# Moving the cache_win row copies from the FFN to the projections, and re-ordering the start of a trunk layer

## The chip, the cores and the metric

The kernel runs on one core of a Trainium2 chip. The core has five engines that work side by side: TensorE (PE, matmuls), VectorE (DVE), ScalarE (ACT), GpSimd (POOL) and SyncE (SP, which here issues most DMAs). Each engine takes its instructions in order; engines wait for each other by semaphores. The metric is the device time of one execution in microseconds (us), the median over runs.

## The reference

One inference step of one trunk layer, for a prompt of 512 tokens and 8 samples of 4 tokens each, 544 tokens in all, width 1024, in float32:

```
adaLN modulation from silu(c) @ w_ada                     # per sequence
h = modulate(rmsnorm(x))
p = h @ w_in       # conv B, C, x_in | q | 3 kinds of k,v | gate | merge
y_a = B * conv3(C * x_in)
y_b = compressed + selected + sliding-window attention, gated per head
x = x + g1 * (merge(y_a, y_b) @ w_out)
x = x + g2 * swiglu(modulate(rmsnorm(x)))                 # 2816 wide
y = rmsnorm(x)
```

The samples read paged caches of 1024 past rows. The compressed branch passes blocks of 32 cached rows through a small MLP called phi. Outputs are y, the new cache rows, and for each sample the window cache `new_win_sample`: the old 512 rows of `cache_win` moved up by four, with four new rows at the end.

## The kernel before, in words

**Precision and linears.** A float32 matrix is used as a pair of float32r matrices, high and low part. A linear is three matmuls per 128 rows of k (`mm3`, L180 to L183): wh with x_hi, wh with x_lo, wl with x_hi. Tokens go in two halves of 288 and 256 columns. Weights arrive as 1 MB slabs of 256 output columns (`slab`, tile `raw`, three buffers); each half of a slab is split by `split`: ACT writes wh (L176), DVE then writes wl (L177). wh and wl have two buffers each, so a split can run while the linear before uses the other buffer, and must wait until the linear two before has ended.

**Order.** The order of instructions on each engine is set by a list scheduler, which models durations and DMAs and picks by time and priority; `tc.issue_after(x)` tells it to place what follows behind x. On the chip the order is then fixed. SP's queue is in order too: a DMA that waits for data holds up every DMA behind it, and each waits for the completion of the one eight before it.

**Stages.** (1) `wake`: transposes of the identity on PE while the first data arrive. (2) A loop of 16 steps n: `cmp_gather` reads 1 MB of cache_cmp pages by an indirect DMA on POOL's queue, two steps ahead; `cmp_copy` re-orders it on DVE (two copies to `gt2`); `cmp_T` transposes it on PE and splits it into xh (ACT) and xl (DVE); `cmp_M` multiplies by the phi weights. Those weights (`rphi`) are split in quarters by `phi_split` into wph (ACT) and wpl (DVE). Between the steps stand the adaLN slabs (`mod_slab`), the token rows (`x_rows`), the norm and `modulate`. (3) `kv_type` 0, 1, 2: six slabs of k and v projections. Of each half, ACT copies the result to `kvT`; `kv_post`, which follows one half later, transposes it on PE (`kvt`, `sps`), copies it to `stage` and `rows`, splits k into kh and kl and stores all these; at the end of types 1 and 2 ACT spreads the v rows into `vext`. `cmp_prompt` stands between types 1 and 2 (results `pps`, then `ph1` on ACT). (4) One gate slab (`gT`) and the q projections (tiles `rq`, results qh and ql, stored to `q_dr`). (5) The convolution and the samples' attention, whose selected rows are gathered from cache_sel in 2 MB pieces (`sraw`); (6) merges and prompt attention; (7) the output projection; (8) the FFN: a loop over c2 in which each pass takes a w_gate slab and a w_up slab, and leaves silu(gate) * up in `ffg`, split by ACT and DVE into f_hi and f_lo; (9) the down projection and the final norm.

**The cache rows.** `win_shift(b)` copies 508 rows of one sample from cache_win to new_win_sample, a DMA of 1 MB from DRAM to DRAM on SP's queue that touches no engine. The eight of them stand in the FFN loop, one behind the slabs of each pass c2 = 1 to 8 (L1338, called at L1348).

Of the kernel before, what the change touches and what calls it, by code (L numbers as in the profile page):

```python
# [9 lines left out]
F32 = mybir.dt.float32  # L10
# [9 lines left out]
KC = 8  # L20
TP = 512
# [4 lines left out]
DEC_B = 8  # L26
# [73 lines left out]
def build(tc, a, o):  # L100
    nc = tc.nc
    sync, act, dve, pool, pe = nc.sync, nc.scalar, nc.vector, nc.gpsimd, nc.tensor
# [28 lines left out]
    def nm(s):  # L131
        uid[0] += 1
        return f"{s}_{uid[0]}"
# [28 lines left out]
    last_slab = [None]  # L162
# [223 lines left out]
    perow = wphip.tile([32, 128], F32, name="perow")  # L386
    rws = []
# [26 lines left out]
    def wake():  # L414

        p = tp_ps("wake")
        for n in range(44):
            pe.transpose(p[:, (n % 4) * 128:(n % 4) * 128 + 128], ident, ident)
# [71 lines left out]
    gts.append(cmp_gather(0, 1))  # L490
# [6 lines left out]
    for j in range(4):  # L497
        sync.dma_start(xr[j], a["x_prompt"][j * 128:(j + 1) * 128, :])
# [34 lines left out]
    for n in range(16):  # L533
# [9 lines left out]
        if n == 0:  # L543
            phi_split(1, 0)
        if n < 3:
            for v in range(2):
                phi_split(v, n + 1)
        with tc.issue_after(last_x[0].ins), tc.issue_after(last_x[1].ins):
            if n == 0:
                pp = tp_ps("pep")  # L550
                pe.transpose(pp[:, 0:32], perow, ident[0:32, 0:32])
                dve.tensor_copy(peT[:, 0:32], pp[:, 0:32])
                vp = tp_ps("vp")
                pe.transpose(vp[:, 0:104], vrow, ident[0:104, 0:104])
                dve.tensor_copy(vec, vp[:, 0:104])
# [14 lines left out]
            if 1 <= n < 9:  # L570
                mod_slab(n - 1)
            if 3 <= n < 7:
                x_rows(n - 3)
            if n == 7:
                iv = inv_from_sums(ss1, xp)
                iv2 = xp.tile([128, 3], F32, name="iv2")
                dve.tensor_copy(iv2[:, 0:2], iv[:, 0:2])
                dve.tensor_copy(iv2[:, 2:3], iv[:, 4:5])
                invs = (inv_bcast(iv2, 0, xp), inv_bcast(iv[:, 2:4], 1, xp))
            if n == 9:  # L580
                modp.pop()()
                make_A(n1T, sc1, A1)
                mods = [modulate(xT, invs[hf], A1, sh1, hh_, hl_, hf, xp) for hf in range(2)]
            if 9 <= n < 13:
                for g_ in mods:
                    for _ in range(2):
                        next(g_)
        if n == 13:
            with tc.issue_after(last_slab[0].ins):
                sync.dma_start(x_dr, xT.rearrange("p k n -> p (k n)"))  # L590
            xst.close()
# [6 lines left out]

    def kv_type(ty, rp, x32=None):
        sps = acc_ps(nm("sps"))  # L600
        for v in range(2):
            sl = slab(a["w_in"], C_KV + ty * 512 + v * 256)
            stage = rp.tile([128, 4, 256], F32, tag="stage", bufs=2, name=nm("stage"))
# [97 lines left out]
    pool.memset(qbd, 0.0)  # L701
    for gp in range(2):
        for rp_ in range(2):
# [5 lines left out]
            for r2 in range(2):  # L709
# [3 lines left out]
                hl = [rp.tile([128, TP], F32R, tag=f"q{n}", bufs=2, name=nm("q" + n)) for n in "hl"]  # L713

# [10 lines left out]
                for n in range(2):  # L725
                    sync.dma_start(q_dr[gp][n][:, r * TP:(r + 1) * TP], hl[n].bitcast(F32))
# [609 lines left out]
    def win_shift(b):  # L1336
        flat = lambda z: z.rearrange("t w -> (t w)").rearrange("(p f) -> p f", p=128)
        sync.dma_start(flat(o["new_win_sample"][b, 0:508, :]), flat(a["cache_win"][b, 4:512, :]))  # L1338

# [5 lines left out]
    for c2 in range(1, FC // 2):  # L1345
        sg, su = slab(a["w_gate"], c2 * 256), slab(a["w_up"], c2 * 256)
        if c2 <= DEC_B:
            with tc.issue_after(last_slab[0].ins):  # L1348
                win_shift(c2 - 1)
# [110 lines left out]
```

## Time and profile before

| | |
|---|---|
| median of 3 runs | 1359.87 us (1359.06 to 1360.66) |
| profiled execution | 1358.56 us |
| its span | 1356.7 us |
| PE busy | 1315.6 us (97%) |
| DVE, ACT, POOL busy | 653.4, 538.8, 69.5 us |
| mean granted clock of PE | 0.991 |
| DMA traffic | 193.56 MB, 143 GB/s on average |

The span runs from the first to the last instruction that the profiler recorded; the time has 1.9 us around it. Busy times are of one engine each and overlap. In rows of the timeline the columns are the start, the duration, engine, line, operation, output and inputs, and in brackets the idle time of that engine just before and what ended it. In rows of windows they are start and end, length, busy time (and count) of PE, its weight loads, DVE, ACT and POOL, then the granted clock, the mean busy share of the DMA engines and GB/s.

### The profile page before, as it was taken

How to read it: one execution, taken by the hardware profiler on the slowest of the kernel's cores; microseconds unless marked ns; L12 is line 12 of the kernel's file. 1: busy time of each engine (PE TensorE's matmuls, PEld its weight loads, DVE VectorE, ACT ScalarE, POOL GpSimd, SP SyncE). 2: the span in 40 equal slices, each digit the busy share in tenths (PEclk: the TensorE clock that was granted, in tenths of full speed). 3: DMA queues.
4: the chain of work that ended last, by engine and by line, in shares of the span. 5: the costliest groups of instructions: out<-in, count | busy, mean ns of one | idle time of the engine just before them, and what ended most of it. 6: DMA issues, size and time to landing. Idle time of an engine off the chain costs nothing.

```text
span 1356.7 us, 25742 instructions
## 1 busy us (share of the span) xinstructions
PE 1315.6 (97%) x10884; PEld 1213.6 (89%) x10884; DVE 653.4 (48%) x1570; ACT 538.8 (40%) x1066; POOL 69.5 (5%) x123
## 2 busy tenths in 40 slices
PE   6999999999999999999999999999998999999997
PEld 5787799999999998998777778999998999999997
DVE  4457522244455454327667666657333232323335
ACT  3445333433333335226677666425222222222223
POOL 2001040000111010001000000000000000000000
PEclk7999999999999999999999999999999999999998
DMA  8785123953555443843637337422352243133321
GB/s 265 276 292 178 63 79 112 321 161 127 187 179 223 158 156 126 205 124 127 170 109 192 109 100 205 137 75 94 106 174 93 93 155 94 56 86 86 86 63 66
DMA packets 138024, 193.56 MB, mean 143 GB/s; under 512 B 4817, under 2 KB 124761, under 8 KB 132918
## 3 DMA queue, kind: packets, MB, share of 16 engines
q1 hardware_dynamic: 133302, 149.98, 35.8%
q0 software_dynamic: 4608, 41.95, 8.4%
q8 instruction: 85, 1.39, 0.4%
q14 instruction: 29, 0.24, 0.1%
HBM read 174.47 MB, written 25.76 MB: 148 GB/s over the span
## 4 chain that ended last, share of the span: by engine, by line
PE 94%; DVE 2%; ACT 1%; DMA 1%; issue 1%; SPq 0%; POOL 0%; ACTq 0%; POOLq 0%; DVEq 0%
PE lin L181 19%; PE lin L183 19%; PE lin L182 19%; PE dn L181 3%; PE dn L182 3%; PE dn L183 3%; PE acc L1145 3%; PE ptp L1151 3%; PE phi L458 2%; PE phi L460 2%; PE phi L459 2%; PE xt L444 2%; PE modp L229 2%; PE kt L862 2%; PE sp L1120 1%; PE sp L1121 1%
## 5 line engine op out<-in xcount | busy, mean ns | idle before, releaser
L181 PE MATMUL lin<-h_hi,wh 128*128 128x288 f32 (+1 forms) x1648 | 479.6, 291 | 11.5 <-ACT wh L176 11.5
L183 PE MATMUL lin<-h_hi,wl 128*128 128x288 f32 (+1 forms) x1648 | 473.3, 288 | 2.4 <-DVE wl L177 2.4
L182 PE MATMUL lin<-h_lo,wh 128*128 128x288 f32 (+1 forms) x1648 | 474.8, 289 | 0.0
L181 PEld LDWEIGHTS lin<-h_hi,wh 128*128 128x128 f32 x1648 | 311.1, 189 | 22.0 <-ACT wh L176 12.7
L183 PEld LDWEIGHTS lin<-h_hi,wl 128*128 128x128 f32 x1648 | 309.5, 188 | 4.1 <-DVE wl L177 3.8
L182 PEld LDWEIGHTS lin<-h_lo,wh 128*128 128x128 f32 x1648 | 310.7, 189 | 0.5
L177 DVE TENSOR_TENSOR wl<-raw,wh 128x1024 fp32r<-128x1024 f32 x132 | 158.5, 1205 | 217.6 <-ACT wh L176 217.3
L176 ACT ACTIVATE wh<-raw 128x1024 fp32r<-128x1024 f32 x132 | 137.1, 1043 | 276.3 <-PE lin L182 186.0
L181 PE MATMUL dn<-f_hi,wh 128*128 128x256 f32 (+1 forms) x352 | 101.9, 290 | 0.0
L182 PE MATMUL dn<-f_lo,wh 128*128 128x256 f32 (+1 forms) x352 | 101.3, 288 | 0.0
L183 PE MATMUL dn<-f_hi,wl 128*128 128x256 f32 (+1 forms) x352 | 101.0, 287 | 0.0
L1127 ACT ACTIVATE P<-P,nms 128x512 f32<-128x512 f32 (+3 forms) x128 | 70.6, 555 | 18.8 <-DVE nms L1126 18.1
L1126 DVE CUSTOM_DVE_ANT_0 P<-sp,ta 128x512 f32<-128x512 f32 (+3 forms) x128 | 57.6, 482 | 31.1 <-PE sp L1114 23.5
L183 PEld LDWEIGHTS dn<-f_hi,wl 128*128 128x128 f32 x352 | 66.3, 188 | 0.0
L181 PEld LDWEIGHTS dn<-f_hi,wh 128*128 128x128 f32 x352 | 66.2, 188 | 0.0
L182 PEld LDWEIGHTS dn<-f_lo,wh 128*128 128x128 f32 x352 | 66.2, 188 | 0.0
L1302 DVE TENSOR_TENSOR ffg<-lin,ffg 128x288 f32<-128x288 f32 (+1 forms) x44 | 19.4, 441 | 84.0 <-PE lin L183 84.0
L458 PE MATMUL phi<-xh,wph 128*128 128x512 f32 x128 | 54.1, 423 | 4.3 <-ACT xh L446 4.3
L459 PE MATMUL phi<-xh,wpl 128*128 128x512 f32 x128 | 51.9, 406 | 0.0
L460 PE MATMUL phi<-xl,wph 128*128 128x512 f32 x128 | 51.4, 403 | 0.0
L447 DVE TENSOR_TENSOR xl<-xt,xh 128x512 fp32r<-128x512 f32 x64 | 41.2, 684 | 17.1 <-ACT xh L446 16.9
L446 ACT ACTIVATE xh<-xt 128x512 fp32r<-128x512 f32 x64 | 34.8, 595 | 36.5 <-PE xt L444 35.6
(372 smaller groups left out, 2133.5 us busy)
## 6 DMA issues: line engine op xcount, KB each, us to landing
raw<-in_w_in SPq DMA_DIRECT2D x26, 1024.0 KB, 6.3
raw<-in_w_ada SPq DMA_DIRECT2D x24, 1024.0 KB, 6.0
raw<-in_w_gate SPq DMA_DIRECT2D x11, 1024.0 KB, 5.5
raw<-in_w_up SPq DMA_DIRECT2D x11, 1024.0 KB, 5.3
wraw<-in_cache_win POOLq DMA_DIRECT2D x8, 1024.0 KB, 6.9
raw<-in_w_down SPq DMA_DIRECT2D x8, 1024.0 KB, 5.6
out_new_win_sample<-in_cache_win SPq DMA_DIRECT2D x8, 1016.0 KB, 7.5
rq<-in_w_in SPq DMA_DIRECT2D x8, 512.0 KB, 6.8
```

Source lines behind the costliest of these rows:

```text
L176: act.activation(oh, view, AF.Copy)
L177: dve.tensor_sub(ol, view, oh.bitcast(F32))
L181: pe.matmul(p, lhsT=wh[:, k, :], rhs=xh, start=start, stop=False)
L182: pe.matmul(p, lhsT=wh[:, k, :], rhs=xl, start=False, stop=False)
L183: pe.matmul(p, lhsT=wl[:, k, :], rhs=xh, start=False, stop=stop)
L447: last_x[1] = dve.tensor_sub(xlb[v][:, lp * 512:lp * 512 + 512], p, xo.bitcast(F32))
L458: pe.matmul(po, lhsT=w_h, rhs=mh, start=first, stop=False)
L459: pe.matmul(po, lhsT=w_l, rhs=mh, start=False, stop=False)
L460: pe.matmul(po, lhsT=w_h, rhs=ml, start=False, stop=last)
L1126: dve.tensor_tensor_reduce(out=t[:, 0:n], in0=sps[br], in1=t_dist[:, 512 - n:512], scale=-hs, scalar=3e38, op0=ALU.add, op1=ALU.min, accum ...
L1127: act.activation(t[:, 0:n], t[:, 0:n], AF.Exp, scale=-1.0, bias=nms[:, c:c + 1], accum_out=sums[:, c:c + 1])
L1145: pe.matmul(acc[br * 64:br * 64 + 64, :], lhsT=vtok[br][:, j, g * 64:(g + 1) * 64], rhs=pts_[br], start=(j == 0), stop=False)
```

## The change

At the start: forty more identity transposes in `wake`; the second gather of cache_cmp is issued behind a small POOL copy that waits for the first one's data; the phi splits of a step are tied behind the splits of the gathered rows of that step; the x_prompt rows are loaded in steps 3 to 6 instead of at the start; the adaLN slabs, the token rows, the norm and modulate move two to four steps later. Further on: the copies win_shift(0) to (5) are issued behind the six k and v slabs, (6) and (7) behind stores of the q projections, and none in the FFN.

```diff
@@ -384,6 +384,7 @@
     sel = wphip.tile([128, 1], F32, name="sel")
     pbias = wphip.tile([128, 2], F32, name="pbias")
     perow = wphip.tile([32, 128], F32, name="perow")
+    gate = wphip.tile([128, 1], F32, name="gate")
     rws = []
 
     def phi_load(v):
@@ -414,7 +415,7 @@
     def wake():
 
         p = tp_ps("wake")
-        for n in range(44):
+        for n in range(84):
             pe.transpose(p[:, (n % 4) * 128:(n % 4) * 128 + 128], ident, ident)
 
     xhb = [gat.tile([128, 1026], F32R, name=f"xh{j}") for j in range(2)]
@@ -487,15 +488,14 @@
     sync.dma_start(perow, a["pe_cmp"].rearrange("v l d -> (v l d)").rearrange("(k p) -> k p", p=128))
     sync.dma_start(w2, a["w_phi2"].rearrange("v p d -> p v d"))
     phi_load(1)
-    gts.append(cmp_gather(0, 1))
+    with tc.issue_after(pool.tensor_copy(gate, gts[0][:, 0:1]).ins):
+        gts.append(cmp_gather(0, 1))
     for r0, nme, n in ((24, "b_ada", 48), (0, "norm1", 8), (8, "norm2", 8), (16, "norm_f", 8), (72, "b_conv", 8), (80, "w_conv", 24)):
         s = a[nme]
         s = s.rearrange("a b -> (a b)") if len(s.shape) == 2 else s
         sync.dma_start(vrow[r0:r0 + n, :], s.rearrange("(k p) -> k p", p=128))
     sync.dma_start(xs, a["x_sample"])
     sync.dma_start(strow, a["state_conv"])
-    for j in range(4):
-        sync.dma_start(xr[j], a["x_prompt"][j * 128:(j + 1) * 128, :])
 
     dve.tensor_reduce(sel, ident.rearrange("p (a b) -> p b a", b=32)[:, 0, :], axis=AX.X, op=ALU.add)
     dve.memset(peT[:, 32:64], 0.0)
@@ -540,12 +540,12 @@
             if pend is not None:
                 cmp_step(*pend)
             pend = (bp, qt, v)
-        if n == 0:
-            phi_split(1, 0)
-        if n < 3:
-            for v in range(2):
-                phi_split(v, n + 1)
         with tc.issue_after(last_x[0].ins), tc.issue_after(last_x[1].ins):
+            if n == 0:
+                phi_split(1, 0)
+            if n < 3:
+                for v in range(2):
+                    phi_split(v, n + 1)
             if n == 0:
                 pp = tp_ps("pep")
                 pe.transpose(pp[:, 0:32], perow, ident[0:32, 0:32])
@@ -567,25 +567,28 @@
                     phi_bias(v)
             if n == 2:
                 x_rows(4)
-            if 1 <= n < 9:
-                mod_slab(n - 1)
-            if 3 <= n < 7:
-                x_rows(n - 3)
-            if n == 7:
+            if 3 <= n < 11:
+                mod_slab(n - 3)
+            if 6 <= n < 10:
+                x_rows(n - 6)
+            if n == 10:
                 iv = inv_from_sums(ss1, xp)
                 iv2 = xp.tile([128, 3], F32, name="iv2")
                 dve.tensor_copy(iv2[:, 0:2], iv[:, 0:2])
                 dve.tensor_copy(iv2[:, 2:3], iv[:, 4:5])
                 invs = (inv_bcast(iv2, 0, xp), inv_bcast(iv[:, 2:4], 1, xp))
-            if n == 9:
+            if n == 11:
                 modp.pop()()
                 make_A(n1T, sc1, A1)
                 mods = [modulate(xT, invs[hf], A1, sh1, hh_, hl_, hf, xp) for hf in range(2)]
-            if 9 <= n < 13:
-                for g_ in mods:
-                    for _ in range(2):
-                        next(g_)
-        if n == 13:
+                steps = [g_ for _ in range(KC) for g_ in mods]
+            if n >= 11:
+                for _ in range(4 if n == 11 else 3):
+                    next(steps.pop(0))
+        if 3 <= n < 7:
+            with tc.issue_after(last_slab[0].ins):
+                sync.dma_start(xr[n - 3], a["x_prompt"][(n - 3) * 128:(n - 2) * 128, :])
+        if n == 15:
             with tc.issue_after(last_slab[0].ins):
                 sync.dma_start(x_dr, xT.rearrange("p k n -> p (k n)"))
             xst.close()
@@ -596,10 +599,16 @@
     outs_p = (o["new_cmp_prompt"], o["new_sel_prompt"], o["new_win_prompt"])
     outs_s = (o["new_cmp_sample"], o["new_sel_sample"])
 
+    def win_shift(b):
+        flat = lambda z: z.rearrange("t w -> (t w)").rearrange("(p f) -> p f", p=128)
+        sync.dma_start(flat(o["new_win_sample"][b, 0:508, :]), flat(a["cache_win"][b, 4:512, :]))
+
     def kv_type(ty, rp, x32=None):
         sps = acc_ps(nm("sps"))
         for v in range(2):
             sl = slab(a["w_in"], C_KV + ty * 512 + v * 256)
+            with tc.issue_after(last_slab[0].ins):
+                win_shift(ty * 2 + v)
             stage = rp.tile([128, 4, 256], F32, tag="stage", bufs=2, name=nm("stage"))
             for gp in range(2):
                 dst = rp.tile([128, NT], F32, tag="kvT", bufs=2, name=nm("kvT"))
@@ -699,6 +708,7 @@
     dve.tensor_copy(gtok, p[:, 0:192].rearrange("p (i f) -> p i f", i=4))
 
     pool.memset(qbd, 0.0)
+    last_q = [None]
     for gp in range(2):
         for rp_ in range(2):
             t = raw_tile("rq")
@@ -711,6 +721,9 @@
                 ch = gp * 4 + r
                 w = split(tv[:, :, :, r2 * 64:(r2 + 1) * 64], perm=lambda z: z.rearrange("p k (g f) -> p k g f", g=2))
                 hl = [rp.tile([128, TP], F32R, tag=f"q{n}", bufs=2, name=nm("q" + n)) for n in "hl"]
+                if ch in (1, 3):
+                    with tc.issue_after(last_q[0].ins):
+                        win_shift(6 + ch // 2)
 
                 def ev(hf, p):
                     src = p[:, TS:288] if hf == 0 else p
@@ -723,7 +736,7 @@
                             dve.tensor_scalar_mul(qbd[pr, :, gp, gg * 16 + r * 4:gg * 16 + r * 4 + 4], p[pr, 0:TS].rearrange("p (b t) -> p b t", t=4), 0.125)
                 linear(w, h, ev)
                 for n in range(2):
-                    sync.dma_start(q_dr[gp][n][:, r * TP:(r + 1) * TP], hl[n].bitcast(F32))
+                    last_q[0] = sync.dma_start(q_dr[gp][n][:, r * TP:(r + 1) * TP], hl[n].bitcast(F32))
     rst.close()
     p0.close()
 
@@ -1333,10 +1346,6 @@
             if hf == 0:
                 next(nh)
             ffn_up(c, g_, w[1], hf)
-    def win_shift(b):
-        flat = lambda z: z.rearrange("t w -> (t w)").rearrange("(p f) -> p f", p=128)
-        sync.dma_start(flat(o["new_win_sample"][b, 0:508, :]), flat(a["cache_win"][b, 4:512, :]))
-
     wxst.close()
     n2st.close()
     f6b = mkpool(f6st, "f6b", side="right")
@@ -1344,9 +1353,6 @@
         ffn_tiles(f6b, c)
     for c2 in range(1, FC // 2):
         sg, su = slab(a["w_gate"], c2 * 256), slab(a["w_up"], c2 * 256)
-        if c2 <= DEC_B:
-            with tc.issue_after(last_slab[0].ins):
-                win_shift(c2 - 1)
         for cc in range(2):
             c, g_ = c2 * 2 + cc, ffg()
             for v, fn in ((sg, lambda w, hf: ffn_gate(g_, w, hf)), (su, lambda w, hf: ffn_up(c, g_, w, hf))):
```

What the scheduler makes of it shows in the order of rows on each engine. First ACT at the end of the k and v projections of type 1, from the last evacuations of that type to the first slab of type 2 (wh_287 and wh_296 are its two halves). Before:

```order
L606 ACTIVATE kvT_261_2136<-lin_264_2141 128x288
L176 ACTIVATE wh_287_2363<-raw_284_2359 128x1024
L606 ACTIVATE kvT_261_2136<-lin_265_2167 128x256
L606 ACTIVATE kvT_269_2208<-lin_272_2213 128x288
L176 ACTIVATE wh_296_2458<-raw_284_2359 128x1024
L606 ACTIVATE kvT_269_2208<-lin_273_2239 128x256
L140 ACTIVATE stage_260_2135<-kvt_274_2265 128x4x128
L663 ACTIVATE ph1_278_2312<-pps_277_2309,pbias_161 128x4x31
L663 ACTIVATE ph1_282_2355<-pps_281_2352,pbias_161 128x4x31
```

And now:

```order
L615 ACTIVATE kvT_261_2182<-lin_265_2213 128x256
L615 ACTIVATE kvT_269_2254<-lin_272_2259 128x288
L615 ACTIVATE kvT_269_2254<-lin_273_2285 128x256
L672 ACTIVATE ph1_278_2358<-pps_277_2355,pbias_161 128x4x31
L140 ACTIVATE stage_260_2181<-kvt_274_2311 128x4x128
L140 ACTIVATE rows_292_2475<-sps_241_2030 32x512
L655 ACTIVATE vext_96<-rows_292_2475 32x2048
L672 ACTIVATE ph1_282_2401<-pps_281_2398,pbias_161 128x4x31
L176 ACTIVATE wh_287_2410<-raw_284_2405 128x1024
L176 ACTIVATE wh_296_2505<-raw_284_2405 128x1024
```

Both splits of the slab stood between the evacuations of the slab before; now they stand behind all evacuations, the phi result, stage, rows and vext.

SP at the same place, where raw_284, raw_303 and raw_319 are the last three slabs of this stage (the third is the gate). Before:

```order
L167 DMA raw_284_2359<-in_w_in 128x8x256
L632 DMA out_new_cmp_prompt<-stage_215_1720 128x4x256
L167 DMA raw_303_2528<-in_w_in 128x8x256
L640 DMA out_new_cmp_sample<-rows_250_2059 32x512
L632 DMA out_new_cmp_prompt<-stage_228_1848 128x4x256
L628 DMA k_dr0h_122<-kh_257_2126 128x512
L628 DMA k_dr0l_123<-kl_258_2127 128x512
L167 DMA raw_319_2667<-in_w_in 128x8x128
```

And now:

```order
L167 DMA raw_284_2405<-in_w_in 128x8x256
L604 DMA out_new_win_sample<-in_cache_win 16x16256
L641 DMA out_new_sel_prompt<-stage_260_2181 128x4x256
L645 DMA v_dr0_126<-stage_260_2181 128x1024
L649 DMA out_new_sel_sample<-rows_292_2475 32x512
L637 DMA k_dr0h_122<-kh_301_2568 128x512
L637 DMA k_dr0l_123<-kl_302_2569 128x512
L167 DMA raw_303_2575<-in_w_in 128x8x256
L604 DMA out_new_win_sample<-in_cache_win 16x16256
```

The slab raw_303 was issued behind the first store of type 0; now it stands behind the stores of type 1 and the k rows of type 2's first half (kh_301, kl_302).

ACT at a boundary of two passes late in the FFN loop, where wh_1720 and wh_1724 are splits of the next gate and up slabs. Before:

```order
L1297 ACTIVATE ffg_1708_11671<-lin_1711_11676 128x288
L1297 ACTIVATE ffg_1708_11671<-lin_1712_11702 128x256
L211 ACTIVATE f_hi7_10742<-ffg_1708_11671 128x288
L211 ACTIVATE f_hi7_10742<-ffg_1708_11671 128x256
L176 ACTIVATE wh_1720_11794<-raw_1717_11788 128x1024
L176 ACTIVATE wh_1724_11850<-raw_1718_11790 128x1024
L1297 ACTIVATE ffg_1719_11793<-lin_1722_11798 128x288
```

And now:

```order
L1310 ACTIVATE ffg_1708_11718<-lin_1711_11723 128x288
L176 ACTIVATE wh_1720_11840<-raw_1717_11835 128x1024
L1310 ACTIVATE ffg_1708_11718<-lin_1712_11749 128x256
L211 ACTIVATE f_hi7_10792<-ffg_1708_11718 128x288
L176 ACTIVATE wh_1724_11896<-raw_1718_11837 128x1024
L211 ACTIVATE f_hi7_10792<-ffg_1708_11718 128x256
L1310 ACTIVATE ffg_1719_11839<-lin_1722_11844 128x288
```

wh_1720 moved ahead of the second evacuation and of both f_hi.

DVE at the start, where gt2_6 and gt2_7 come from the first gather, gt2_14 from the second, and xl0 and xl1 from the first. Before:

```order
L397 TENSOR_TENSOR wpl0_156<-rphi_2_180,wph0_154 128x2x256 x4
L436 COPY gt2_6_254<-gt_3_182 128x1024
L436 COPY gt2_7_256<-gt_3_182 128x1024
L397 TENSOR_TENSOR wpl1_157<-rphi_4_189,wph1_155 128x2x256 x4
L447 TENSOR_TENSOR xl0_168<-xt_9_260,xh0_166 128x512
L447 TENSOR_TENSOR xl0_168<-xt_10_267,xh0_166 128x512
L447 TENSOR_TENSOR xl1_169<-xt_11_274,xh1_167 128x512
L447 TENSOR_TENSOR xl1_169<-xt_12_281,xh1_167 128x512
```

And now:

```order
L398 TENSOR_TENSOR wpl0_156<-rphi_2_181,wph0_154 128x2x256
L437 COPY gt2_6_292<-gt_3_183 128x1024
L437 COPY gt2_7_294<-gt_3_183 128x1024
L437 COPY gt2_14_351<-gt_5_193 128x1024
L448 TENSOR_TENSOR xl0_169<-xt_9_298,xh0_167 128x512
L448 TENSOR_TENSOR xl0_169<-xt_10_305,xh0_167 128x512
L448 TENSOR_TENSOR xl1_170<-xt_11_312,xh1_168 128x512
L448 TENSOR_TENSOR xl1_170<-xt_12_319,xh1_168 128x512
L398 TENSOR_TENSOR wpl1_157<-rphi_4_190,wph1_155 128x2x256
```

The copy of the second gather stands ahead of the four xl of the first, and the splits wpl of the second weight have moved behind them.

## The prediction

> **What bounds the kernel now.** I read the page first, then the waits of the FFN stretch, its windows, and the rows at one stalled boundary.
>
> ```profile
> span 1356.7 us, 25742 instructions
> PE 1315.6 (97%) x10884; PEld 1213.6 (89%) x10884; DVE 653.4 (48%) x1570; ACT 538.8 (40%) x1066; POOL 69.5 (5%) x123
> ...
> PE 94%; DVE 2%; ACT 1%; DMA 1%; issue 1%; SPq 0%; POOL 0%; ACTq 0%; POOLq 0%; DVEq 0%
> ```
>
> TensorE (PE) is busy for 97% of the span and carries 94% of the chain that ended last. The change removes none of PE's matmuls but adds 40 small ones at the start, so time can move only where PE waits or runs at a lower clock. Of the 41 us that PE is idle, the FFN stretch holds a named part:
>
> ```profile
> PE lin L181 <- ACT wh L176: 11.5, 6, 1.9
> PE lin L183 <- DVE wl L177: 2.4, 5, 0.5
> ...
> 956.60:980.84 24.24, 24.24 (x194) 24.24 (x194) 8.26 (x12) 7.11 (x12) 0.00 (x0) 1.00 0.37 131
> 1005.03:1032.08 27.05, 24.65 (x194) 24.24 (x193) 8.26 (x12) 7.11 (x12) 0.00 (x0) 1.00 0.35 117
> 1113.38:1141.44 28.06, 26.15 (x194) 25.66 (x194) 8.26 (x12) 7.10 (x12) 0.00 (x0) 0.94 0.34 113
> 1005.03:1168.54 163.51, 149.62 (x1154) 147.06 (x1153) 49.53 (x72) 42.63 (x72) 0.00 (x0) 0.99 0.33 110
> ```
>
> The first pair are waits (total us, times, longest). The windows run from one issue of a w_up slab to the next, one pass of the c2 loop each; the last row spans six passes. An early pass takes 24.24 us with PE busy throughout. The later six take 163.51 us, 27.25 each, for the same instructions. At one of these boundaries:
>
> ```profile
> 1021.34 0.42 ACT L211 ACTIVATE f_hi<-ffg 128x256 fp32r<-128x256 f32 x1 [2.30 <-DVE ffg L1302]
> 1021.66 1.99 ACT L176 ACTIVATE wh<-raw 128x1024 fp32r<-128x1024 f32 x2
> ...
> 1022.75 0.40 PE L181 MATMUL lin<-h_hi,wh 128*128 128x288 f32 x1 [1.91 <-ACT wh L176]
> 1024.01 0.40 PE L183 MATMUL lin<-h_hi,wl 128*128 128x288 f32 x1 [0.49 <-DVE wl L177]
> ```
>
> ACT's f_hi of the previous tile stands ahead of the split (wh) that PE needs; PE waits 1.91 and 0.49 us. It is a matter of order on ACT, not of data: the slab has long landed.
>
> **Terms of the change.**
>
> *FFN.* The eight 1 MB win_shift copies leave this loop, and with them the scheduler puts wh_1720 ahead of the f_hi pair at all six late boundaries, the pattern that the early passes have. Each pass should then take 24.24: 163.51 − 6 × 24.24 = 18.1, so **−18.1 us**. Its cover is the same matmuls that hide the split in the early passes.
>
> *K, v and q projections.* The copies stand here now, one behind each slab, and the scheduler pays for them: on ACT the splits fall behind the work of the previous slab, and on SP's in-order queue slabs fall behind stores that wait for compute. The prices:
>
> ```profile
> L176 ACT ACTIVATE wh<-raw 128x1024 fp32r<-128x1024 f32 x16 | 16.9, 1059 | 29.0 <-PE lin L182 29.0
> ...
> L646 ACT ACTIVATE vext<-rows 32x2048 f32<-32x2048 f32 x2 | 3.8, 1914 | 0.1
> L140 ACT ACTIVATE stage<-kvt 128x512 f32<-128x512 f32 x6 | 3.5, 592 | 0.0
> L211 ACT ACTIVATE kh<-kvT 128x512 fp32r<-128x512 f32 x4 | 2.5, 626 | 0.0
> ...
> L140 ACT ACTIVATE rows<-sps 32x512 f32<-32x512 f32 x2 | 1.1, 571 | 0.0
> ...
> L663 ACT ACTIVATE ph<-pps,pbias 128x124 f32<-128x124 f32 x2 | 0.8, 400 | 6.4 <-DVE pps L660 6.4
> ```
>
> S1: lin_2414 needs wh_287, which now stands behind rows_292 (it waits PE's last transposes), vext_96 and ph1_282. PE has nothing else. From PE's end: 0.57 + 1.91 + 0.40 + 1.06 = 3.94, with releases about 4.1, and then 0.49 for wl as in the FFN row: **+4.6**. It is certain to within one microsecond, because these are durations in a fixed order.
>
> S3: lin_2721 needs wh_320, behind stage_304 (partly under PE's transposes), rows_325 and vext: 0.57 + 1.91 + 1.06 = 3.54, some 0.45 of the stage, 0.49 for wl: **+4.5**.
>
> S2: lin_2584 needs wh_306 from raw_2575. Its issue now stands on SP behind k_dr0h and k_dr0l of the slab just computed, with a 1 MB copy ahead in the same queue, and the second 2 MB gather of cache_sel on POOL's queue beside it.
>
> ```profile
> 236.03 0.37 ACT L606 ACTIVATE kvT<-lin 128x256 f32<-128x256 f32 x1
> ...
> 240.07 0.32 SPq L628 DMA_DIRECT2D k_dr0l<-kl  x1
> ...
> 240.70 0.41 ACT L606 ACTIVATE kvT<-lin 128x288 f32<-128x288 f32 x1 [1.38 <-PE lin L183]
> ...
> 247.24 0.41 ACT L606 ACTIVATE kvT<-lin 128x288 f32<-128x288 f32 x1 [1.51 <-PE lin L183]
> ...
> out_new_sel_prompt<-stage SPq DMA_DIRECT2D x1, 512.0 KB, 4.7
> ...
> out_new_win_prompt<-stage SPq DMA_DIRECT2D x1, 512.0 KB, 11.1
> ...
> sraw<-in_cache_sel,ixs POOLq DMA_INDIRECT x2, 11.5
> ...
> raw<-in_w_in SPq DMA_DIRECT2D x26, 1024.0 KB, 6.3
> ```
>
> In the run before, k_dr0l goes out 4.4 us after its linear's end (240.07 + 0.32 − 236.03); I take 4 for raw_2575. A slab lands in 6.3 us at the median; but of two equal stores, the one that met the sraw gather took 11.1 instead of 4.7. With 11.1 the split ends 4 + 11.1 + 1.06 = 16.2 after that linear's end. PE has the other half of the slab as cover, 247.24 − 240.70 = 6.5, and about 1 of transposes: 16.2 − 7.6 = **+8.6**. Lower end: ACT's order alone, 0.37 + 0.63 + 0.59 + 1.06 = 2.7. Upper end: 13 for the landing, 10.5. I take the contended row, since the copy and the gather are both in flight there.
>
> S4: rq_2793 is late too and gates wh_327, behind which the table load stands: 0 to 1.3, **+0.3**, since SP issues it before S3 ends.
>
> S5, at the start of the convolution:
>
> ```profile
> 319.63 1.28 ACT L828 ACT_TABLE_LOAD   x1
> 323.02 0.35 ACT L828 ACTIVATE px<-sxs,n 128x63 f32<-128x63 f32 x1 [2.11 <-DVE n L791]
> ...
> 325.62 0.41 PE L834 MATMUL imp<-px,tb 128*128 128x64 f32 x2 [0.72 <-POOL ncv L770]
> ```
>
> There wh_437 now stands ahead of this table load and px, and it waits for the end of a linear to get its buffer back. imp then waits 1.06 + 1.28 + 0.35 and some 0.55 of read and releases, 3.25, instead of 0.72: **+2.5**.
>
> The two copies in the q projections stand behind q_dr stores; no weight slab behind them is needed within 20 us, and their 2 MB are hidden under the linears: 0.
>
> *The clock.* A stall can cost more than itself:
>
> ```profile
> 1100.50:1103.90 3.40, 1.65 (x14) 1.44 (x13) 1.18 (x3) 1.25 (x2) 0.00 (x0) 1.00 0.00 0
> 1127.80:1131.20 3.40, 1.49 (x14) 1.28 (x12) 1.04 (x4) 1.46 (x3) 0.00 (x0) 1.00 0.00 0
> 1131.20:1134.60 3.40, 3.40 (x13) 3.12 (x14) 2.30 (x2) 0.85 (x1) 0.00 (x0) 0.50 0.00 0
> ```
>
> A 3.4 us window with PE busy for 1.49 was followed by one at half the granted clock; one with 1.65 wasn't. That drop made its pass 28.06 instead of the 27.05 of the stalled pass above: 1.0. A whole window at half rate loses 1.7. S1, S2, S3 and S5 idle for longer than 1.91 each: 4 × 1.3 = **+5.2** (2 to 8). [...]
>
> *The start.*
>
> ```profile
> 13.05 3.68 PE L444 MATMUL xt<-ident,gt 128*128 128x128 f32 x16 [4.97 <-DVE gt L436]
> 21.02 0.79 PE L458 MATMUL phi<-xh,wph 128*128 128x512 f32 x1 [4.29 <-ACT xh L446]
> ...
> 12.30 1.29 DVE L436 COPY gt<-gt 128x1024 f32<-128x1024 f32 x2 [0.64 <-DMA gt<-in_cache_cmp,ixc]
> ...
> 8.30 0.97 POOL L428 DMA_INDIRECT gt<-in_cache_cmp,ixc  x1 [0.16 <-issue]
> ...
> 18.29 2.19 ACT L396 ACTIVATE wph<-rphi 128x512 fp32r<-128x512 f32 x4 [7.60 <-DMA rphi<-in_w_phi]
> ...
> 11.60:25.20 13.60, 7.86 (x26) 6.17 (x27) 6.94 (x13) 4.13 (x8) 1.46 (x2) 0.50 1.03 347
> ```
>
> The first phi waits for wph, which ACT splits only when the second rphi lands at 18.29. After the change xh stands ahead of that split, and the longer wake keeps the clock up until the first transposes, so those take half of 3.68 and end near 15.0. But on DVE the copy gt_14 of the second gather now stands ahead of the xl that the phi matmuls need, and that gather is issued only once the first has landed, about 12.4 (DVE's copy at 12.30) instead of 8.30. With the DMA engines full (share 1.03) its 1 MB lands near 18; xl follows at 18.7 and PE resumes at 19.4 instead of 21.02, two phi matmuls ahead. That is 1.6 + 0.5: **−2.1**, from −0.3 (a landing at 20) to −5.6 (the clock also stays up over 15 to 22, worth up to 3.5). x_prompt, mod_slab, norm and modulate move later inside a loop where PE is the bound and the slabs have slack: 0, bounded at ±1.
>
> Sum: −18.1 − 2.1 + 4.6 + 8.6 + 4.5 + 0.3 + 2.5 + 5.2 = +5.5. The profiled execution took 1358.56, 1.3 under the median of the runs, 1359.87; so 1364.1 for the execution and **1365.4** for the median. A change of 0.2%, 2.7 us, is about what a measurement of this kernel can tell from none.
>
> **Rivals.**
>
> R1, not slower: the slab of S2 is not held up by the gather. Speaking for it, 6.3 us at the median; against it, the 11.1 row. S2 falls to its floor of 2.7 and the sum to −0.4: 1359.5. The sum goes under +2.7 once S2 is below 5.8; slower is then wrong. 20%.
>
> [...]
>
> R3, the start yields all it aims at (−5.6), with the clock up and the gather in early: sum +2.0, 1361.9; with R1 beside it, −3.9, 1356. 8%, and 5% for the pair or other gains together.
>
> R4, worse: S2 at 10.5, drops at 8, S4 at 1.3 and nothing at the start: +13 and 1372. 12%.
>
> **How the numbers follow.** Forecast 45%, own range 1362 to 1369; R1 20%, R2 10%, R3 with its pair 13%, R4 12%. The range 1355 to 1372 leaves some 8% beyond either end together with unknown terms. Faster by over 2.7 us: the pair in R3, a third of the low side of R1, 0.17. Within: most of R1, R2 and R3, 0.22. Slower: forecast, R4 and the rest, 0.61.
>
> **What would show it.** Right: w_up issues 24.2 apart all through the FFN; PE idle rows of 4 us ahead of lin <- wh twice near 230 to 262 and a longer one between, each followed by a window at half clock; imp waiting 3 us; first phi matmuls near 15 and the rest from 19.4. Wrong: raw<-in_w_in there landing in 6 us or less (R1), full clock behind the stalls (R2), PE without idle from 12 to 25 (R3), or the FFN passes still at 27.

## The result: 14 us slower, and the profile after

The changed kernel takes 1373.62 us (1372.96 to 1376.80) against 1359.46 (1357.87 to 1360.66): a ratio of 1.0109, interval 1.0090 to 1.0129. The direction was forecast; the size was not (1365.4, range to 1372). The profiled execution took 1374.03 us, 15.5 more than the one before. The head of its page, and its chain:

```profile
span 1371.9 us, 25813 instructions
PE 1328.0 (97%) x10924; PEld 1225.9 (89%) x10924; DVE 654.2 (48%) x1570; ACT 539.4 (39%) x1066; POOL 69.6 (5%) x124
...
PE 93%; DMA 3%; DVE 2%; ACT 1%; issue 1%; SPq 0%; POOL 0%; ACTq 0%; DVEq 0%
```

PE is as busy as before, in share; the chain now has 3% of DMA in it. Two windows of the changed kernel hold exactly the instructions of two windows of the kernel before: the stretch from late in the first k, v slabs to the first step of the samples' attention, and six passes of the FFN loop. First the changed kernel, then the one before for the first stretch:

```profile
167.04:355.22 188.18, 166.88 (x1313) 162.74 (x1313) 53.00 (x96) 59.19 (x93) 16.80 (x28) 0.94 0.53 172
1038.69:1183.81 145.12, 145.12 (x1154) 145.12 (x1153) 49.53 (x72) 42.62 (x72) 0.00 (x0) 1.00 0.28 88
```

```profile
165.20:325.62 160.42, 158.87 (x1313) 156.33 (x1313) 51.24 (x93) 57.05 (x91) 16.80 (x28) 1.00 0.50 162
```

The same 1313 matmuls take 27.8 us more: PE idles 21.3 instead of 1.5, and is busy for 8.0 more at a granted clock of 0.94. The same 1154 of the FFN take 18.4 us less than the 163.51 shown ahead, with no idle time at all. The four places where PE idles for long in the first stretch, in PE's timeline:

```profile
235.06 0.50 PE L181 MATMUL lin<-h_hi,wh 128*128 128x288 f32 x1 [3.98 <-ACT wh L176]
261.08 0.61 PE L181 MATMUL lin<-h_hi,wh 128*128 128x288 f32 x1 [9.21 <-ACT wh L176]
280.62 0.61 PE L181 MATMUL lin<-h_hi,wh 128*128 128x288 f32 x1 [3.96 <-ACT wh L176]
...
355.22 0.66 PE L847 MATMUL imp<-px,tb 128*128 128x64 f32 x2 [3.32 <-issue]
```

These are S1, S2, S3 and S5 of the prediction. The bracket is the idle time and its end; the duration of the first matmul behind it, 0.50 to 0.66 us instead of 0.40, is the lower clock. Windows of 3.4 us behind S2 show how long that lasts:

```profile
258.60:262.00 3.40, 0.92 (x4) 0.92 (x4) 0.94 (x1) 2.00 (x2) 0.00 (x0) 0.50 0.72 292
262.00:265.40 3.40, 3.40 (x16) 3.25 (x16) 1.42 (x2) 0.00 (x0) 0.00 (x0) 0.50 0.14 54
265.40:268.80 3.40, 3.40 (x27) 3.40 (x27) 0.00 (x0) 0.41 (x1) 0.00 (x0) 0.92 0.02 5
```

PE is back at 261.08, and runs at half rate until shortly into the third window: 4.9 us, not one window. The last windows at half clock behind S1, S3 and S5 are

```profile
235.21:238.63 3.42, 3.42 (x14) 3.16 (x15) 2.19 (x2) 0.75 (x1) 0.00 (x0) 0.50 1.04 446
283.00:286.41 3.41, 3.41 (x16) 3.41 (x16) 1.16 (x1) 2.23 (x2) 0.00 (x0) 0.50 1.17 291
358.10:361.51 3.41, 3.41 (x17) 3.41 (x17) 2.80 (x9) 1.19 (x2) 0.53 (x3) 0.50 0.19 62
```

Behind S1 PE, back at work, runs at half clock for 3.4 us, behind S2 for 4.9, behind S3 for 5.8 and behind S5 for 6.3: 20.4 us in all. Half of that is 10.2.

The start, in the changed kernel:

```profile
13.13 1.91 PE L445 MATMUL xt<-ident,gt 128*128 128x128 f32 x16
...
12.72 1.25 POOL L429 DMA_INDIRECT gt<-in_cache_cmp,ixc  x1 [0.16 <-DVE gt L437]
...
19.70 0.69 DVE L437 COPY gt<-gt 128x1024 f32<-128x1024 f32 x1 [6.58 <-DMA gt<-in_cache_cmp,ixc]
...
21.05 0.80 PE L461 MATMUL phi<-xl,wph 128*128 128x512 f32 x1 [5.54 <-DVE xl L448]
```

The transposes of the first gather run at full clock, 1.91 us instead of 3.68. But the second gather's copy stands on DVE at 19.70, the xl of the first gather behind it, and PE waits 5.54 us, and goes on no sooner than in the kernel before (21.02). The clock falls behind this wait, and once more later. Changed kernel, then the one before:

```profile
21.05:27.00 5.95, 5.95 (x17) 4.46 (x18) 4.40 (x9) 0.00 (x0) 0.00 (x0) 0.50 0.02 8
37.24:40.65 3.41, 3.41 (x45) 2.87 (x37) 0.45 (x2) 0.00 (x0) 0.00 (x0) 0.50 0.03 7
```

```profile
21.02:25.25 4.23, 4.23 (x10) 2.93 (x11) 3.52 (x7) 1.40 (x3) 0.00 (x0) 0.50 1.00 375
```

At 165 us of the kernel before the same matmul comes 1.8 us later in this profile.

So the profile's account is: start +1.8, idle +19.8 and clock +8.0 up to the attention, the clock behind S5 +2.9, a wait for a late cache_sel gather in the attention +1.15, FFN −18.4: +15.2 of span.

### The profile page after: what moved, and what is told of

The parts are those of the page before. It is cut to its first block, busy times and chain, and to the rows that moved or that the text cites. A ratio compares the mean times of both kernels' runs of the same rounds, so it can differ in the third digit from the quotient of the medians.

```text
span 1371.9 us, 25813 instructions
## 1 busy us (share of the span) xinstructions
PE 1328.0 (97%) x10924; PEld 1225.9 (89%) x10924; DVE 654.2 (48%) x1570; ACT 539.4 (39%) x1066; POOL 69.6 (5%) x124
## 4 chain that ended last, share of the span: by engine, by line
PE 93%; DMA 3%; DVE 2%; ACT 1%; issue 1%; SPq 0%; POOL 0%; ACTq 0%; DVEq 0%
PE lin L181 19%; PE lin L182 18%; PE lin L183 18%; PE dn L182 3%; PE dn L181 3%; PE dn L183 3%; PE acc L1158 3%; PE ptp L1164 3%; PE phi L461 2%; PE phi L459 2%; PE phi L460 2%; PE xt L445 2%; PE modp L229 2%; PE kt L875 2%; PE sp L1133 1%; DMA gt<-in_cache_cmp,ixc 1%
## 5 line engine op out<-in xcount | busy, mean ns | idle before, releaser
L1164 PEld LDWEIGHTS ptp<-ident,P 128*128 128x128 f32 x320 | 35.7, 141 | 10.9 <-issue 8.9
```

The costliest lines, as they stand in the source:

```text
L1164: pe.transpose(tp[:, r * 128:(r + 1) * 128], P[br, r][:, 128 * j:128 * j + 128], ident)
```

## The experiments

Where a kernel is said to have the start of before, or the copies of before, that part is word for word the kernel before. Times are medians, and ratios stand against the kernel before, run beside it. e_ladder and the three runs of the long stall are single executions, of which only rows of the trace are read.

### The two parts alone

e_start has the changed start with the copies back in the FFN:

```diff
-            with tc.issue_after(last_slab[0].ins):
-                win_shift(ty * 2 + v)
...
+        if c2 <= DEC_B:
+            with tc.issue_after(last_slab[0].ins):
+                win_shift(c2 - 1)
```

> The re-ordered start alone; the eight copies stand in the FFN loop as before, and so do the orders of ACT there and in the projections. Theory A (from the profile of after, where the same matmul stands 1.8 us later than before all through 146 to 228 us): the start costs 1.8 us, time 1361.3 against 1359.5. Theory B (my prediction): the start gains 2.1, 1357.4, and the 1.8 comes from the copies that follow. By A the second gather's data arrive near 19.7 again and PE idles some 5.5 us ahead of the first matmul with xl.

Measured 1363.22, ratio 1.0024 (1.0014 to 1.0034): the start loses about 3.3 us, more than A's 1.8. PE idles 4.94 ahead of the first matmul with xl, as A has it. B is out. The point at 165 us, though, came 0.3 earlier than before in this profile: in kernels with one and the same start that point wanders by some 4 us from trace to trace (further on, one and the same w_up slab is issued at 953.95 in held_ffn and at 957.91 in e_nocopies), so a single profile doesn't size this part; the timed runs do.

e_copies is the other half: the start of before, the copies in the projections.

> The moved copies alone, with the start of before. Theory A: the rest of the change, 15.2 - 1.8 = +13.4 us, 1372.9; four stalls of PE near 4.0, 9.2, 4.0 and 3.3 us, each followed by a low clock. Theory B (start and copies interact, for instance by the state of the DMA queues): less than 11 or more than 16.

Measured 1366.03, ratio 1.0041 (1.0026 to 1.0056), about +5.6 and not +13.4. Theory B was right: the parts interact. Three stalls are there (10.11, 3.95 and 3.31 us), S1 is not: with the early start the scheduler puts wh_287 right behind stage_260, ahead of rows_292 and vext_96. S1 needs both parts. The two parts alone add up to 8.9 us, the whole change to some 14; S1's 3.98 us and the drop of the clock behind it are about the difference. The long one:

```profile
255.32 0.61 PE L181 MATMUL lin<-h_hi,wh 128*128 128x288 f32 x1 [10.11 <-ACT wh L176]
```

Without any copy:

> Before, with the eight copies left out everywhere (508 of the 512 rows of each sample's window cache aren't written). Theory A (all that the copies cost in the FFN is the order that the scheduler chooses with them): every pass of the loop takes 24.2 us, time 1359.5 - 18.4 = 1341. Theory C (the copies' traffic itself slows PE or the slabs somewhere): more than 18.4 is gained, below 1339.

Measured 1341.28, ratio 0.9857 (0.9840 to 0.9874): −18.5 us, the time that A has. This run takes the traffic of the copies away together with the order that they bring; held_ffn below keeps the traffic.

### What a drop of the clock costs

e_ladder repeats one split, in place, a growing number of times:

```diff
-        act.activation(oh, view, AF.Copy)
+        for _ in range(again + 1):
+            act.activation(oh, view, AF.Copy)
```

> The kernel without copies, and in the passes c2 = 2 to 10 of the FFN the first split of the pass writes its wh 4 to 10 times more (the same values), which makes PE wait from about 0 to 6 us once a pass. What a pass takes beyond 24.2 us, less the idle time of PE in it, is the price of the clock. Theory A (a drop lasts from PE's return to the end of the first window of 3.4 us that PE fills): no price at idle times under about 1.7, and 1.7 to 3.4 us above it, whatever the length. Theory B (my prediction's term): about 1.3 each. [...]

PE's rows behind the stalls of 3 us and more (the passes with 4 and 5 repeats idled for 0.5 and 0.8 us and kept the clock):

```profile
1026.14 0.40 PE L183 MATMUL lin<-h_hi,wh 128*128 128x288 f32 x1 [3.01 <-ACT wh L178]
...
1054.92 0.40 PE L183 MATMUL lin<-h_hi,wh 128*128 128x288 f32 x1 [4.10 <-ACT wh L178]
...
1086.41 0.61 PE L183 MATMUL lin<-h_hi,wh 128*128 128x288 f32 x1 [5.18 <-ACT wh L178]
...
1118.64 0.61 PE L183 MATMUL lin<-h_hi,wh 128*128 128x288 f32 x1 [6.27 <-ACT wh L178]
...
1152.81 0.61 PE L183 MATMUL lin<-h_hi,wh 128*128 128x288 f32 x1 [7.36 <-ACT wh L178]
...
1182.62 0.61 PE L183 MATMUL lin<-h_hi,wh 128*128 128x288 f32 x1 [3.01 <-ACT wh L178]
...
1213.84 0.61 PE L183 MATMUL lin<-h_hi,wh 128*128 128x288 f32 x1 [4.10 <-ACT wh L178]
```

From each row to the next there are the same 192 matmuls. Less the idle time at the end, these six stretches take 24.68, 26.31, 25.96, 26.81, 26.80 and 27.12 us; an undisturbed pass takes 24.19. The first stretch is at full clock, and its 0.5 is the price of filling up; less that, a drop cost 1.3 to 2.4 us. One idle time of 3.01 us dropped the clock and was the dearest of all, the other, as long, didn't drop it at all. So it is not the length alone.

In this trace the granted clock changes only at instants that are whole multiples of 3.413 us apart; so it does in those of the kernel before (11.60, 25.25, 1131.17, 1134.58) and of the changed one (235.21, 238.63, 255.69, 265.93 and others). Here it falls at 1055.55, 1086.27, 1116.99, 1147.71, 1181.84 and 1212.56, and rises at 1058.96, 1089.68, 1123.82, 1157.95, 1188.67 and 1219.39. Cut at this grid, the two stalls of 3.01 us read

```profile
1021.42:1024.83 3.41, 1.71 (x15) 1.51 (x13) 0.88 (x2) 3.38 (x6) 0.00 (x0) 1.00 0.00 0
1024.83:1028.25 3.42, 2.11 (x14) 1.92 (x15) 2.55 (x3) 1.26 (x3) 0.00 (x0) 1.00 0.00 0
...
1178.43:1181.84 3.41, 1.18 (x10) 0.97 (x9) 1.01 (x3) 3.38 (x5) 0.00 (x0) 1.00 0.00 0
1181.84:1185.25 3.41, 2.63 (x11) 2.64 (x12) 2.60 (x3) 0.72 (x1) 0.00 (x0) 0.50 0.00 0
```

The stall that kept the clock is shared by two windows, in which PE is busy for 1.71 and 2.11 us. The other leaves only 1.18 in one window, and the next one is at half clock. In the traces of the kernel before and the changed one, cut the same way from 160 to 1300 us, the clock fell behind the five windows of full clock with PE busy for 1.50 us or less (1.50 before; 0.15, 0.00, 0.50 and 0.63 in the changed one), and behind none of the others, of which the least busy has 1.70; in e_tied below it fell behind 1.44 and 1.61. (At 37.24 us of the changed kernel it also fell behind a window with 2.07.) In both traces it came back only at the end of a window with PE busy for 3.41 us or more, the whole of it, and not behind one with 2.87 (354.68 to 358.09 of the changed kernel). So in the ladder PE runs at half clock for the rest of the window in which it returns, and often for one more: 3.3 to 6.1 us, and it paid 0.4 to 0.5 us for each of these.

A is right on how long a drop lasts, its sizes are somewhat high, and it is wrong that 1.7 us of idle time suffices wherever it falls. B's 1.3 is the low end.

### The start

> The re-ordered start alone, as in e_start, but the second gather isn't held behind the first one's data; the orders of ACT, DVE and PE are those of e_start. Theory A (the start loses because the gated gather lands near 19.7 and four xl stand behind its copy on DVE): the gather lands near 16, PE idles 2 instead of 5 us ahead of the first matmul with xl, and the time falls by 2 to 4 us against e_start (1363.2), to 1359 to 1361. Theory B (the adaLN slabs, rows and norm that moved later make the loss): no difference to e_start, 1363.

Measured 1359.35, ratio 1.0003 (0.9991 to 1.0015). The time fell by A's size, but not by A's mechanism: the second gather, issued at 8.63, still landed near 19.1, and PE still waited 4.71 us for xl. Its point at 165 us came 1.2 us late, no better than in e_start. What makes the medians of these two differ by 3.9 us is left open; it isn't shown in the start.

> e_start with 44 identity transposes instead of 84. Theory A (PE waits for xl at 21 us anyway, so a warm clock for the first transposes buys nothing): same as e_start, 1363.2 within 1. Theory B (my prediction: the warm transposes are worth 1.8): 1365.

Measured 1357.70, ratio 0.9999 (0.9985 to 1.0013): neither theory. It is 5.5 us faster than e_start by the medians, 3.4 by the ratios; with 44 transposes the scheduler stands the copy of the second gather behind the xl and the wpl on DVE, and the wait of PE for xl is gone. Whether that copy or the transposes did it, xlfirst tells: 84 transposes, and

```diff
+        if n == 1:
+            with tc.issue_after(last_x[1].ins):
+                g2t = cmp_copy(gts[n])
```

> e_start with its 84 identity transposes, and the copy of the second gather tied behind the xl of the first on DVE; nothing else moves. Theory A (the DVE copy is the cause, the number of transposes only led the scheduler to place it): the idle time of some 5 us ahead of the first matmul with xl is gone, time 3 to 6 below e_start (1363.2), 1357 to 1360. Theory B (the 40 transposes themselves cost time on PE): as e_start.

Measured 1354.84, ratio 0.9967 (0.9956 to 0.9979), 8.4 below e_start. The idle time is gone, so A's cause is shown; the gain is larger than its 3 to 6. Its DVE and PE rows:

```profile
14.58 2.49 DVE L448 TENSOR_TENSOR xl<-xt,xh 128x512 fp32r<-128x512 f32 x4 [0.78 <-ACT xh L447]
...
21.28 1.29 DVE L437 COPY gt<-gt 128x1024 f32<-128x1024 f32 x2 [2.14 <-DMA gt<-in_cache_cmp,ixc]
...
15.69 0.40 PE L461 MATMUL phi<-xl,wph 128*128 128x512 f32 x1
```

The first matmul with xl starts at 15.69 instead of 21.05. The copy isn't the whole of it: e_wake44 has the same order on DVE, and xlfirst is still 3 to 4 us below it, with intervals that don't touch. The transposes of the first gather, in xlfirst and in e_wake44:

```profile
13.26 2.13 PE L445 MATMUL xt<-ident,gt 128*128 128x128 f32 x16 [0.33 <-DVE gt L437]
```

```profile
12.53 3.58 PE L445 MATMUL xt<-ident,gt 128*128 128x128 f32 x16 [4.02 <-DVE gt L437]
```

With 44 transposes PE idles for 4.02 us ahead of them, and they take 3.58 us, close to the 3.68 of the kernel before, whose granted clock there is 0.50. So the longer wake seems to be worth something of its own once nothing takes it back; the two weren't run side by side.

The same copy in the changed kernel:

> The changed kernel with 44 identity transposes instead of 84; DVE then has the copy of the second gather behind the xl of the first, and ACT's order in the projections stays as changed. Theory A (the start loses by that one copy on DVE): PE doesn't wait for xl near 20 us, and the time falls by 3 to 6, to 1368 to 1371. Theory B (the start's loss comes from the later slabs, rows and norm): 1373.6 within 1.5.

Measured 1370.74, ratio 1.0088 (1.0069 to 1.0107), 2.9 below the changed kernel and at the small end of A, but the intervals of the two overlap, so the time alone doesn't settle it. PE no longer waits for xl; the four stalls stay (3.98, 9.99, 3.96 and 3.31).

### The long stall

> e_copies (the copies moved, the start of before), with the second cache_sel gather held back until the gate slab has landed; otherwise its order of ACT and SP. The long stall ahead of the fifth k and v slab's second use was 10.1 us there. Theory A (the slab lands late because the 2 MB gather runs beside it): the slab lands in 6 to 7 us and the stall falls to 4 to 6. Theory B (the late issue and the copies in the same queue do it): the stall stays at 9 or more.

The stall stayed at 10.05. But the gather beside the slab was the first one, which stood where it was: issued 235.56, landed by 247.70, while the slab, issued at 240.38, was split at 251.43. So this run tells nothing against the gather, only nothing for it. (The late gather stalled the gate's linear, and the time of 1372.61 isn't read.)

> e_copies without the copy that stands right behind that slab in SP's queue (508 rows of one sample aren't written). Theory A (gather): the slab still lands in 10 us or more, stall 9 or more. Theory B (the copy beside it): the slab lands in 8 us or less, and the stall falls by 3 or more.

The stall stayed at 10.13, and the slab, issued at 238.88, still landed 11.1 us later: the copy beside it does nothing.

```profile
250.03 2.01 ACT L176 ACTIVATE wh<-raw 128x1024 fp32r<-128x1024 f32 x2 [8.11 <-DMA raw<-in_w_in]
...
251.14 0.61 PE L181 MATMUL lin<-h_hi,wh 128*128 128x288 f32 x1 [10.13 <-ACT wh L176]
```

Then both gathers were held back, by a small POOL copy that reads the gate slab:

> e_copies with both 2 MB gathers of cache_sel issued only once the gate slab has landed; ACT's order is that of e_copies. In s2_lategather only the second was held back, but the one in flight beside the slab there was the first (issued 235.56, landed 247.5). Theory A (the gather beside it makes the slab late): the slab now lands in 7 us or less instead of 11, and the stall falls from 10 to about 5. Theory B (the late issue, the copies and stores in the same queue): landing 10 or more, stall 9 or more. The samples' attention will wait for the late gathers, which adds to the end time and isn't read.

SP's issue, ACT's split and PE behind it:

```profile
239.24 0.45 SPq L167 DMA_DIRECT2D raw<-in_w_in  x1
...
245.61 2.00 ACT L176 ACTIVATE wh<-raw 128x1024 fp32r<-128x1024 f32 x2 [2.63 <-DMA raw<-in_w_in]
...
246.72 0.61 PE L181 MATMUL lin<-h_hi,wh 128*128 128x288 f32 x1 [4.66 <-ACT wh L176]
```

The slab lands 6.4 us after its issue instead of 11 to 12, and the stall falls from 10 to 4.66. The gather beside it costs half of the stall. The other half I put down to the late issue, behind stores that wait for compute; no run takes that away by itself.

In the changed kernel the same pair reads:

```profile
245.88 1.03 POOL L814 DMA_INDIRECT sraw<-in_cache_sel,ixs  x1 [1.01 <-issue]
...
248.26 0.45 SPq L167 DMA_DIRECT2D raw<-in_w_in  x1
...
259.97 2.00 ACT L176 ACTIVATE wh<-raw 128x1024 fp32r<-128x1024 f32 x2 [7.19 <-DMA raw<-in_w_in]
```

### Order on ACT alone

e_tied keeps the copies where the change has them, but ties the work behind a half to the next split:

```diff
-                while kvp:
-                    kvp.pop(0)()
+                with tc.issue_after(last_split[0].ins):
+                    while kvp:
+                        kvp.pop(0)()
```

> The changed kernel with the work that follows a half of a k or v slab tied behind the split of the next half on ACT: wh_287 then stands ahead of rows and vext, wh_320 ahead of rows and vext; SP's order stays. Theory A (two of the stalls are ACT's order and nothing else): the first falls from 4.0 to under 1, the third from 4.0 to about 1.5, the long one stays at 9; without the two drops of the clock the time is 8 to 12 us below that of the changed kernel: 1362 to 1366. Theory B (the slabs themselves are late there): the stalls stay, 1373.

Measured 1367.26, ratio 1.0054 (1.0034 to 1.0074), 6.4 below the changed kernel. PE's idle times there are now

```profile
234.69 0.40 PE L183 MATMUL lin<-h_hi,wh 128*128 128x288 f32 x1 [1.97 <-ACT wh L178]
...
260.54 0.61 PE L183 MATMUL lin<-h_hi,wh 128*128 128x288 f32 x1 [8.95 <-ACT wh L178]
...
277.70 0.40 PE L183 MATMUL lin<-h_hi,wh 128*128 128x288 f32 x1 [1.41 <-ACT wh L178]
```

S1 and S3 halve or better, S1 not to under 1 as A had it: on ACT wh now stands behind ph, whose input DVE delivers only at 233.30. The first matmul of 0.40 is still at full clock, but the clock falls just behind it. The next window of the grid, at S1 and at S3:

```profile
235.04:238.45 3.41, 3.37 (x15) 2.99 (x14) 2.08 (x2) 2.93 (x3) 0.00 (x0) 0.50 1.03 351
279.41:282.83 3.42, 3.42 (x16) 3.42 (x15) 1.23 (x1) 2.99 (x3) 0.75 (x3) 0.50 1.13 302
```

The windows ahead of these have PE busy for 1.44 and 1.61 us. So A is right that the two stalls are ACT's order, and wrong that their drops of the clock would go with them: both are there in this trace, and the gain stays under its 8 to 12.

### Where the copies can go

p_ffn issues them on POOL's queue (one word: `pool.dma_start`). The tie to SP's slab doesn't hold a DMA of another queue: the scheduler moves the copies up among the gathers of the first loop, and the trace has them issued from 15.6 to 165.5 us.

> Before, with the eight copies issued on POOL's queue instead of SP's; the scheduler then places them among the gathers of the first loop, and the order of ACT in the FFN and in the projections is the one without copies. Theory A (the copies cost only by the order that SP's queue and the scheduler's model give): the FFN passes take 24.2 us, no stall in the projections, 1341.3 as without copies, plus at most 3 for traffic in the first loop. Theory C (8 MB beside the gathers and slabs of the first loop delay them): over 1345.

Measured 1359.86, ratio 0.9997 (0.9984 to 1.0009): C. In the first loop PE now waits for gathers and for an adaLN slab, as the waits of p_ffn from 30 to 170 us show (us in total, times, longest):

```profile
PE xt L444 <- DVE gt L436: 8.5, 3, 5.9
PE modp L229 <- DMA raw<-in_w_ada: 4.4, 1, 4.4
```

From 30 us to the end of that loop it takes 19.4 us longer, 12.7 of idle time and 6.7 of PE at a lower clock: all that the FFN gains. Whether the traffic delays the gathers, or the copies' place ahead of them in POOL's queue, isn't separated.

> p_ffn with the start of the changed kernel, but 44 identity transposes (as in e_wake44). Theory A: the gain of both parts, 1341.3 less 2 to 4 for the start: 1337 to 1340. Theory B (the start gains nothing that lasts to the end of the first loop): the time of p_ffn within 1.5.

Measured 1346.73, ratio 0.9910 (0.9892 to 0.9928): neither theory's time. With the later slabs of the changed start, one wait of 4.26 us in that loop and one of 1.67 are left of those.

Then a dependence that holds the copies in the FFN:

```diff
-            with tc.issue_after(last_slab[0].ins):
+            with tc.issue_after(pool.tensor_copy(hold, sg[:, 0, 0:1]).ins):
                 win_shift(c2 - 1)
...
-        sync.dma_start(flat(o["new_win_sample"][b, 0:508, :]), flat(a["cache_win"][b, 4:512, :]))
+        pool.dma_start(flat(o["new_win_sample"][b, 0:508, :]), flat(a["cache_win"][b, 4:512, :]))
```

> Before, with the eight copies issued on POOL's queue, each held in its FFN pass by a one-column copy of that pass's gate slab on POOL; the order of ACT is the one without copies. Theory A (the traffic of the copies costs nothing in the FFN; only the order did): passes of 24.2 us, 1341.3 within 1.5. Theory C (the copies beside the slabs delay them there): passes over 24.5, more than 1344.

Measured 1341.07, ratio 0.9867 (0.9851 to 0.9882): A, the time without copies. Six passes, in which four of the copies stand:

```profile
1002.37:1147.45 145.08, 145.08 (x1154) 145.08 (x1153) 49.57 (x72) 42.62 (x72) 5.00 (x8) 1.00 0.36 116
```

All eight copies are issued between 920.5 and 1086.9, and from 920 to 1153 PE waits for 0.3 us in all: in the FFN the copies cost only by the order that their place in SP's queue led to.

> held_ffn with the start of e_wake44 (the changed start, 44 transposes). Theory A: the gain of both, 1336 to 1340, below held_ffn by 2 to 5. Theory B (the start gains nothing that lasts): as held_ffn within 1.5.

Measured 1335.77, ratio 0.9828 (0.9814 to 0.9842): A, 0.2 under its range.

> held_best with 84 identity transposes and the copy of the second gather tied behind xl on DVE, the start of xlfirst. Theory A (with the DVE order put right the longer wake keeps the clock up for the first transposes, worth up to 1.8): 1333 to 1335.5, below held_best (1335.8). Theory B (the forty transposes buy nothing): 1335.8 within 1.5.

Measured 1334.10, ratio 0.9819 (0.9800 to 0.9839). It is the fastest, some 26 us below the kernel before and 39 below the changed one; between A and B it can't be told, since the intervals of the last two overlap widely.

## Why the prediction was right in direction and wrong in size

By its own terms, against the profiled executions (sum +5.5 forecast, +15.5 measured; of the 10.0 between them the clock has 4.7, the start 3.9, a late gather 1.15):

- FFN, −18.1: measured −18.4, by the step named, the split ahead of f_hi. e_nocopies and held_ffn show that nothing but order was in it.
- The idle times S1 4.1, S2 8.6, S3 4.0 and S5 2.5 (the first and third without their wait for wl): measured 3.98, 9.21, 3.96 and 2.60 beyond what was there before. Rows of the kernel before, put into the new order, gave these to 0.6 us. For S2 the contended landing was the right row to take (11.1 forecast, 11.7 seen), and the gather is about half of the cause, as s2_lateboth shows.
- **The clock, +5.2, is the first step that failed.** With the waits for wl (1.0) the prediction had 6.2 behind the four stalls; measured are 8.0 and 2.9, 10.9. I took 1.3 each from a drop that lasted one window. Behind these four stalls PE ran at half clock for 20.4 us, half of which is 10.2; only behind S1 was it one window. The term was mis-sized by leaving out the rest of the window in which PE returns; the ladder shows 1.3 to 2.4 a drop.
- **The start, −2.1, is the second, and of the wrong sign.** 1.8 late in the profile, 3.3 in the timed runs of e_start. The DVE copy ahead of xl was named, but its price came from a landing at 18; it landed at 19.7, and PE went on at 21.05 instead of 19.4. By the prediction's own chain that leaves −0.4. The clock, which stands in this term only as a gain, took more: half clock to 27.00 behind the wait, where the kernel before had it to 25.25, and again from 37.24 to 40.65. What else adds up to 1.8 or 3.3 stays open (e_start_nogate). The wake did give its gain (1.91 instead of 3.68), but the scheduler answered the longer wake with just that copy's place (e_wake44, xlfirst), and the wait behind it took the gain back. The range for this step reached to −0.3 and should have gone above zero, since PE's wait was being traded for another one and not removed.
- Not in the sum: a late cache_sel gather in the attention, 1.15. S4 came to 0.3 at most, as forecast.
- R4, worse, at 1372, was the nearest, priced with wide drops and no gain at the start; it had 12%. Its terms add up to +13.3, which on the median is 1373.2 and not 1372. That it comes so close is partly luck: its S2 of 10.5 and S4 of 1.3 didn't come, and its drops at 8 and its start at nothing were still too small. R1 (a slab that isn't held up) is out by the 11.7; R2, at 10% (full clock behind some of the stalls), by the granted clock of 0.50 behind all four.
- That S1 belongs to the copies was also wrong, though the sum doesn't show it: it appears only with both parts together.

## What to carry to other kernels

A DMA that touches no engine can still cost much, 18 us in this FFN, by what the scheduler does around it; price the order that results, on every engine, before the bytes. Give a transfer that nobody waits for a queue that nobody else's data stand in, and a real dependence that holds it in the stage with room; a mere tie across engines doesn't hold it (1341.07 us in held_ffn, 1359.86 in p_ffn). And price a stall of PE as its length plus the clock, here 1.3 to 2.4 us where it left one 3.413 us window of the clock's grid with PE busy for 1.18 us or less, and 0.5 where it left 1.71 and 2.11.

## What the runs showed that I had not expected

- Two stalls of the same 3.01 us, one with half clock behind it and a price of 2.4, the other at full clock and none.
- A second gather issued 4 us earlier (8.63 in e_start_nogate, 12.72 in the changed kernel) was copied only 0.6 us earlier (19.10 against 19.70).
- Forty transposes of the identity, which nothing waits for, moved a copy on another engine, and with it some 5 us of waiting.
